# Attention scores as plain float32 products on two row groups of TensorE, in place of split float32r parts

## The chip, the cores and the metric

The kernel runs on one core of a Trainium2 chip. The metric is device time in microseconds. The run before was timed three times: 2007.59, 2006.73 and 2007.32 us, median 2007.32.

The engines are called as in the profile: PE is TensorE's matrix products, PEld its weight loads, DVE VectorE, ACT ScalarE, POOL GpSimd, and SP the queue that issues most DMAs.

## What is computed

One inference step of a two-layer backbone for 384 tokens: 256 latent tokens and 128 context tokens, 1024 channels. Each layer has a SwiGLU feed-forward block, a token-mixing block and a second feed-forward block, all with normalisation and modulation from a conditioning vector. The mixing block has a gated spatial branch and an attention branch. The attention branch is the one that changes:

```python
def diff_attention(q, k, v, lam):
    ...
    def block(qi):
        s = jnp.einsum('bqhid,bkhid->bihqk', qi, k).astype(jnp.float32) * scale
        p = jax.nn.softmax(s, axis=-1)
        a = p[:, 0] - lam * p[:, 1]
        return jnp.einsum('bhqk,bkhe->bqhe', a.astype(v.dtype), v)
```

There are 8 heads of 128 channels. A head has two halves `i` of 64 channels. Each half gives its own scores and softmax; the second softmax, times `lam`, is taken from the first. Latent queries see 128 cached context keys and 256 latent keys, 384 in all. Context queries see the 128 context keys alone. Latent queries and keys are turned by a rotary product first.

## The kernel before, in words

Activations are kept transposed, with channels on the partitions and the 384 tokens along the row. Weights stream in from HBM in pairs of chunks of 1 MB, issued by SP (`load_next`). Each 128x1024 chunk is split into two float32r parts, `whi` by ACT (L173) and `wlo` by DVE (L176). A projection (`col_job`) goes over 8 weight tiles of 128x128 and makes three float32r products for each (`mm3`: L226 `whi` by `h_hi`, L227 `wlo` by `h_hi`, L228 `whi` by `h_lo`).

The order of the work is written by hand. A job is a generator that yields after each weight tile. `fill(n)` runs the next n tiles of the queue of jobs.

Attention is cut in 48 units over the two layers: 8 heads by 3 groups of 128 queries. Two of the three groups are latent queries with 384 keys (called long units below), the third is context queries with 128 keys (short units). The table `ORDER` says what runs between the units' phases; `F` entries are fills, so projections of the next heads and of the gates run beside attention:

```python
ORDER = [(c[0], int(c[1:])) for c in "S0 F1 B0 T1 F3 E0 C0 O2 F4 P1 F1 X2".split()]
```

- `phase_s` (S) makes the scores of one unit in a PSUM tile `sc` of two halves with 512 columns each, and DVE takes the maximum (L943, L944). The tile has one buffer.
- `phase_e` (E) is the exponential on ACT (L953). `phase_c` (C) joins the two halves on DVE (L962 to L965).
- `phase_t` (T, L974), `phase_p` (P, L990), `phase_o` (O) and `phase_x` (X, L1013) transpose, multiply by the values, normalise and transpose back, for units one or two steps older.
- B, after the third unit of a head, runs the jobs up to the next head's projections and calls `build` for it.

`q_evac` and `k_evac` take the projections of one head out of PSUM into `qf` and `kf` and apply the rotary product (`rope`, L769 to L772). `k_evac` also loads the cached keys beside them (L785). `build` then splits both into float32r parts, two halves by five operations: four on ACT in all (L802, L804), six on DVE (L803, L805, L807). Tile `qa` holds, for a half, the 64 rows of the high part beside the 64 rows of the low part; `ka` holds the high part of the keys twice; `kl` their low part. So the first score product of a half (L940) goes over 128 rows and the second (L941) over 64:

```python
T.matmul(sc[:, i, 0:nk], lhsT=qa[h][:, i, js], rhs=ka[h][:, i, keys], start=True, stop=False)
T.matmul(sc[:, i, 0:nk], lhsT=qa[h][rows, i, js], rhs=kl[h][rows, keys], start=False, stop=True)
```

Three places with plain float32 products are in the kernel already and are used below for comparison. L990 is the product with the values. L415 (`mod_piece`) and L463 (`mod_piece_v`) make the modulation; they cut the array in four column groups of 32 weight columns by `tile_position`. L415 makes four products, one on each group, for each of 8 channel tiles. L463 makes four products in all, one on each group.

Of the kernel before, what the change touches and what calls it, by code (L numbers as in the profile page):

```python
# [9 lines left out]
F32 = mybir.dt.float32  # L10
F32R = mybir.dt.float32r
AF = mybir.ActivationFunctionType
ALU = mybir.AluOpType
# [25 lines left out]
def hybrid_step(  # L39
# [19 lines left out]

# [1 line left out]
    ident = cp.tile([P, P], F32, name="ident")  # L61
# [22 lines left out]

# [1 line left out]
    # A job is a generator that yields after each 128x128 weight tile. Weights come in pairs of  # L86
    # chunks (1 MB each pair); a chunk is 8 tiles, split into two float32r parts when it is near.
    jobs = []
# [18 lines left out]
    def plan_order():  # L107
        seen = set()
        upto = 0

        def see(key):
            if key not in seen:
                seen.add(key)
                order.append(key)

        for j in jobs:
            for m in j.mods:
                see(m)
            if j.n:
                lim = min(len(chunks), j.first + max(j.n, 1) + W_BUFS - 1)  # L120
                if j.n > W_BUFS:
                    lim = min(len(chunks), j.first + W_BUFS)
                while upto < lim:
                    see(chunks[upto][:-1])
                    upto += 1
                # later chunks of a long job
                while upto < min(len(chunks), j.first + j.n + W_BUFS - 1):
                    see(chunks[upto][:-1])
                    upto += 1
# [27 lines left out]
    def run_later(n=1):  # L157
        # what was put off by some tiles of work, in order
        for e in later:
            e[0] -= n  # L160
        while later and later[0][0] <= 0:
            later.pop(0)[1]()
# [60 lines left out]

# [1 line left out]
    def mm3(ps, w_hi, w_lo, r_hi, r_lo, first, last):  # L225
# [38 lines left out]
    def start_group(keys, rhs, evacs, make):  # L264
        # The first products, while the first modulation comes in by quarters (two k-tiles each).
        q_keys = [[("w_mod0", n, q) for n in range(2)] for q in range(4)]
# [124 lines left out]

    # modulation: one piece (1024 columns) of silu(cond) @ w_mod + b_mod
    def mod_keys(l, pc):
# [11 lines left out]
    def mod_piece(l, pc):  # L405
        # The four column groups of the array work on 256 columns each.
        big = pp.tile([P, 2, 512], F32, tag="sc", name="sc")
# [31 lines left out]
    def mod_piece_v(l, pc):  # L439
        # the products on the vector engine, the sum over partitions on the tensor engine  # L440
        acc0 = sp.tile([P, 1024], F32, tag="KA", name="acc0")
        acc1 = [sp.tile([P, 512], F32, tag=t, name="acc1") for t in ("KL", "kf")]
        parts = [(0, slice(0, 1024), acc0), (1, slice(0, 512), acc1[0]), (1, slice(512, 1024), acc1[1])]
# [37 lines left out]
    class Mods:  # L481
        # modulation pieces cut in steps, put between other jobs
        def __init__(self, pieces=(), pieces_v=()):
# [34 lines left out]

# [1 line left out]
    nst = {}  # L520
# [13 lines left out]
    def rsqrt(v, w, E):  # L534
        # r = v**-0.5, with a Newton step on the engine E
        r = tiny(w, "yr")
# [43 lines left out]
    def make_h(l, i, pc_sh):  # L580
# [9 lines left out]
        def make(kt, ahead=2):  # L590
            # h of k-tile kt; the part that needs no bias runs two tiles ahead
            for k2 in range(kt, min(kt + ahead, KD)):
# [24 lines left out]
    def norm_job(make, mods):  # L617
        # the first products of mods run while the norm is worked out
        steps = [mods.take() for _ in range(3)]
# [18 lines left out]

# [1 line left out]
    def ffn(l, i, w13, w2, mods, first=3):  # L640
# [60 lines left out]

# [1 line left out]
    def mixer(l, mods):  # L703
# [60 lines left out]

        qf, kf, qa, ka, kl, vc = {}, {}, {}, {}, {}, {}

# [7 lines left out]
        def q_evac(h):  # L774
            def e(ps):
                qf[h] = sp.tile([P, NT], F32, tag="qf", name="qf")
                S.activation(out=qf[h], in_=ps, func=AF.Copy)
                rope(qf[h][:, LATS])
            return e

        def k_evac(h):
            # the keys of a head: cached, latent, context
            def e(ps):
                t = sp.tile([P, 512], F32, tag="kf", name="kf")
                nc.sync.dma_start(out=t[:, 0:P], in_=a["cache_k"][l, h])  # L785
                S.activation(out=t[:, P:512], in_=ps, func=AF.Copy)
                nc.sync.dma_start(out=a["new_k"][l, h], in_=t[:, 384:512])
                rope(t[:, P:384])
                kf[h] = t
                if h == 0:  # L790
                    bg.append(lambda: build(0))
            return e

        def build(h):
            # float32r parts: 64 rows of a half of the head, beside them the rows of the other part
            q, k = qf.pop(h), kf.pop(h)
            qa[h] = sp.tile([P, 2, NT], F32R, tag="QA", name="QA")
            ka[h] = sp.tile([P, 2, 512], F32R, tag="KA", name="KA")
            kl[h] = sp.tile([P, 512], F32R, tag="KL", name="KL")
            lower, upper = slice(0, 64), slice(64, 128)  # L800
            for i, own, oth in ((0, lower, upper), (1, upper, lower)):
                S.activation(out=qa[h][own, i, :], in_=q[own, :], func=AF.Copy)  # L802
                V.tensor_copy(out=ka[h][own, i, :], in_=k[own, :])  # L803
                S.activation(out=ka[h][oth, i, :], in_=k[own, :], func=AF.Copy)  # L804
                V.tensor_tensor(  # L805
                    out=qa[h][oth, i, :], in0=q[own, :], in1=qa[h][own, i, :].bitcast(F32), op=ALU.subtract)
                V.tensor_tensor(  # L807
                    out=kl[h][own, :], in0=k[own, :], in1=ka[h][own, i, :].bitcast(F32), op=ALU.subtract)
            vc[h] = sp.tile([P, P], F32, tag="vc", name="vc", bufs=2)
            nc.sync.dma_start(out=vc[h], in_=a["cache_v"][l, h])  # L810

# [15 lines left out]
        def gate_evac(which, f):  # L827
            def e(ps):
# [4 lines left out]
                else:  # L833
                    if f % 2 == 0:
                        tg["t"] = sp.tile([P, 2, NT], F32, tag="QA", name="tg")
                    t = tg["t"][:, f % 2, :]
# [22 lines left out]

        # w_in pairs: u 0-3, zv 4-7, (q,k) 8-15, v 16-19, g_a 20-23, g_b 24-27  # L860
        def wk(pair, half):
# [21 lines left out]
        col_job(wk(8, 1), rhs_h, k_evac(0))  # L883
        # zv and v share a slot, so the spatial gate is through before v is written
        vk = [wk(16 + i // 2, i % 2) for i in range(8)]
# [4 lines left out]

        # what the tensor engine does beside the attention
        side = []
# [4 lines left out]
        while side or hq < NH:  # L897
            # the next head's projections end shortly before its scores
            if hq < NH and (not side or pos + 8 > PER_HEAD * hq - 28):
# [27 lines left out]

# [1 line left out]
        units = [(h, j) for h in range(NH) for j in range(3)]  # L929
        us = {}  # L930

        def phase_s(n):
# [3 lines left out]
            sc = pp.tile([P, 2, 512], F32, tag="sc", name="sc")  # L936
            js = slice(j * P, (j + 1) * P)
            for i in range(2):
                rows = slice(i * 64, (i + 1) * 64)
                T.matmul(sc[:, i, 0:nk], lhsT=qa[h][:, i, js], rhs=ka[h][:, i, keys], start=True, stop=False)  # L940
                T.matmul(sc[:, i, 0:nk], lhsT=qa[h][rows, i, js], rhs=kl[h][rows, keys], start=False, stop=True)  # L941
            mx = tiny(2, "ym")
# [77 lines left out]
        def attention():  # L1020
            nu = len(units)
            for n in range(nu + 3):
                for what, arg in ORDER:
# [6 lines left out]
                    if what == "B":  # L1030
                        h = units[u][0] + 1
                        if units[u][1] == 2 and h < NH:
                            run_until(qk_job[h])
                            build(h)
                        continue
# [16 lines left out]
    def lambdas():  # L1052
        lamb = nst.pop("lamb")
        # -lambda per layer
        lp = tmp(256).rearrange("p (l r d) -> p l r d", l=2, r=2)
# [11 lines left out]

# [1 line left out]
    marks = []  # L1069
# [18 lines left out]
    with tc.manual_schedule():  # L1088
# [23 lines left out]
        run_later(99)  # L1112
        # final norm
        norm_stats0()
# [11 lines left out]
def _cols(w, n0, n):  # L1126
    # (L, 8*128, N) columns n0..n0+n -> (L, n/256, 128, 2*8*128): pairs of column tiles
    L = w.shape[0]
# [4 lines left out]
def _rows(w, n0):  # L1133
    # (L, 1024, N) columns n0..n0+1024 -> (L, 4, 128, 4*512): halves of 512 columns, by 4 k-tiles
    L = w.shape[0]
# [66 lines left out]
```

## Time and profile before

| | |
|---|---|
| median of three timed runs | 2007.32 us |
| span of the profiled execution | 2006.0 us |
| PE busy | 1971.3 us, 98% |
| DVE busy | 1211.9 us, 60% |
| ACT busy | 830.1 us, 41% |
| POOL busy | 149.4 us, 7% |
| moved by DMA | 308.66 MB, 154 GB/s |

The profile is of one execution. Its own time is given as the span from its first to its last instruction, 2006.0 us; no other time stands beside it. The timed median is 1.3 us above that.

The page lists busy time by engine, then 40 slices of the span, then groups of instructions. The trace behind it can be asked for a timeline of one engine, for groups by line and form, and for the busy time of each engine in a stretch. Matmuls overlap in the records, so that the duration of one (0.34 us for 384 columns) is longer than the distance between the starts of two; distances between starts tell the pace. A plain float32 product of two 4-byte operands stands in the trace as two records of PE and two weight loads, a float32r product as one of each.

### The profile page before, as it was taken

To read this page: it belongs to the slowest core of one execution; us is meant where nothing else is said; L and a number is where in the kernel's file an instruction comes from. 1 tells how busy PE (TensorE), PEld (TensorE's weight loads), DVE (VectorE), ACT (ScalarE), POOL (GpSimd) and SP (SyncE) were. 2 spreads that over 40 slices of the span, in tenths; PEclk is the share of its full clock that TensorE was granted. 3 is DMA by queue.
4 is the path that set the end of the run, shared out by engine and by line. 5 is a ranking of instruction groups with operands and counts; after the bars stand their busy time and mean duration, and the time that the engine had idled before them with its cause. 6 is when DMAs were issued, how large, how long until landed. Compare 5 with 4: busy or idle time off the path is not lost. (4 is left out here: it accounts for less than half of the span.)

```text
span 2006.0 us, 28427 instructions
## 1 busy us (share of the span) xinstructions
PE 1971.3 (98%) x11442; PEld 1873.7 (93%) x11442; DVE 1211.9 (60%) x1942; ACT 830.1 (41%) x1484; POOL 149.4 (7%) x407
## 2 busy tenths in 40 slices
PE   7999999999999999999999999999999999999997
PEld 5999998888999999999999999989898999999997
DVE  5757685368874565667556577445688645544433
ACT  4433324446663353333343333253566533533321
POOL 0000000003441000000000000000144300000000
PEclk9999999999999999999999999999999999999999
DMA  8645556533233344545554455453323233533330
GB/s 327 212 154 184 182 224 220 189 121 105 85 111 106 126 166 170 189 168 189 178 181 167 168 189 196 166 180 122 121 76 113 102 123 122 189 124 127 125 124 32
DMA packets 52115, 308.66 MB, mean 154 GB/s; under 512 B 6416, under 2 KB 13968, under 8 KB 15632
## 3 DMA queue, kind: packets, MB, share of 16 engines
q1 hardware_dynamic: 51552, 306.74, 42.7%
q8 instruction: 90, 1.47, 0.3%
q14 instruction: 41, 0.34, 0.0%
q10 hardware_dynamic: 432, 0.11, 0.0%
HBM read 303.16 MB, written 3.67 MB: 153 GB/s over the span
## 5 line engine op out<-in xcount | busy, mean ns | idle before, releaser
L176 DVE TENSOR_TENSOR wlo<-raw,whi 128x1024 fp32r<-128x1024 f32 x424 | 517.7, 1224 | 345.8 <-ACT whi L173 345.7
L226 PE MATMUL mm<-h_hi,whi 128*128 128x384 f32 x2048 | 702.5, 343 | 3.9 <-ACT h_hi L602 3.9
L228 PE MATMUL mm<-h_lo,whi 128*128 128x384 f32 x2048 | 689.1, 336 | 0.6
L227 PE MATMUL mm<-h_hi,wlo 128*128 128x384 f32 x2048 | 688.3, 336 | 0.0
L173 ACT ACTIVATE whi<-raw 128x1024 fp32r<-128x1024 f32 x424 | 444.7, 1052 | 227.7 <-PE mm L228 147.3
L226 PEld LDWEIGHTS mm<-h_hi,whi 128*128 128x128 f32 x2048 | 384.4, 188 | 19.2 <-ACT h_hi L602 6.9
L228 PEld LDWEIGHTS mm<-h_lo,whi 128*128 128x128 f32 x2048 | 384.4, 188 | 2.5 <-DVE h_lo L605 2.4
L227 PEld LDWEIGHTS mm<-h_hi,wlo 128*128 128x128 f32 x2048 | 384.8, 188 | 0.2
L226 PE MATMUL mm<-S,whi 128*128 128x384 f32 x1088 | 370.2, 340 | 0.0
L228 PE MATMUL mm<-S,whi 128*128 128x384 f32 x1088 | 365.7, 336 | 0.0
L227 PE MATMUL mm<-S,wlo 128*128 128x384 f32 x1088 | 365.6, 336 | 0.0
L226 PEld LDWEIGHTS mm<-S,whi 128*128 128x128 f32 x1088 | 204.1, 188 | 6.6 <-issue 6.1
L227 PEld LDWEIGHTS mm<-S,wlo 128*128 128x128 f32 x1088 | 204.2, 188 | 0.0
L228 PEld LDWEIGHTS mm<-S,whi 128*128 128x128 f32 x1088 | 204.1, 188 | 0.0
L383 ACT ACTIVATE S<-t 128x384 fp32r<-128x384 f32 x104 | 54.6, 525 | 318.5 <-DVE t L664 280.8
L455 DVE SCALAR_TENSOR_TENSOR acc<-raw,scond,acc 128x512 f32<-128x512 f32 (+1 forms) x210 | 182.4, 925 | 0.0
L664 DVE TENSOR_TENSOR t<-t,mm 128x384 f32<-128x384 f32 x88 | 48.7, 554 | 122.3 <-PE mm L228 120.5
L538 POOL TENSOR_TENSOR yr<-yv,nhalf 128x3 f32<-128x3 f32 x9 | 7.7, 855 | 1515.1 <-DVE yv L564 1393.9
L656 ACT ACTIVATE t<-mm 128x384 f32<-128x384 f32 x88 | 43.2, 490 | 168.0 <-PE mm L228 167.9
L386 DVE TENSOR_TENSOR S<-t,S 128x384 fp32r<-128x384 f32 x104 | 58.1, 558 | 60.9 <-ACT S L383 60.9
L363 PE MATMUL mm<-whi,h_hi 128*128 128x512 f32 x192 | 77.2, 402 | 1.4 <-ACT S L820 1.4
L364 PE MATMUL mm<-wlo,h_hi 128*128 128x512 f32 x192 | 75.2, 392 | 0.0
(143 smaller groups left out, 1513.0 us busy)
## 6 DMA issues: line engine op xcount, KB each, us to landing
raw<-in_ffn_w SPq DMA_DIRECT2D x132, 1024.0 KB, 4.9
raw<-in_w_mod SPq DMA_DIRECT2D x68, 1024.0 KB, 5.0
raw<-in_w_in SPq DMA_DIRECT2D x56, 1024.0 KB, 4.9
raw<-in_w_branch_a SPq DMA_DIRECT2D x8, 1024.0 KB, 5.0
raw<-in_w_branch_b SPq DMA_DIRECT2D x8, 1024.0 KB, 5.0
raw<-in_w_out SPq DMA_DIRECT2D x8, 1024.0 KB, 4.9
S<-in_w_mod SPq DMA_DIRECT2D x4, 1024.0 KB, 14.7
x<-in_x SPq DMA_DIRECT2D x4, 384.0 KB, 4.2
```

The lines of the kernel that those rows point to most:

```text
L173: S.activation(out=hi, in_=raw, func=AF.Copy)
L176: V.tensor_tensor(out=lo, in0=raw, in1=hi.bitcast(F32), op=ALU.subtract)
L226: T.matmul(ps, lhsT=w_hi, rhs=r_hi, start=first, stop=False)
L227: T.matmul(ps, lhsT=w_lo, rhs=r_hi, start=False, stop=False)
L228: T.matmul(ps, lhsT=w_hi, rhs=r_lo, start=False, stop=last)
L363: T.matmul(ps, lhsT=l_hi[:, kt, ts_], rhs=hi[:, sl], start=first, stop=False)
L364: T.matmul(ps, lhsT=l_hi[:, kt, ts_], rhs=lo[:, sl], start=False, stop=False)
L383: S.activation(out=dst_hi, in_=src, func=AF.Copy)
L386: V.tensor_tensor(out=dst_lo, in0=src, in1=dst_hi.bitcast(F32), op=ALU.subtract)
L455: V.scalar_tensor_tensor(out=acc, in0=src, scalar=s, in1=acc, op0=ALU.mult, op1=ALU.add)
L656: S.activation(out=s, in_=ps, func=AF.Silu)
L664: V.tensor_tensor(out=s, in0=s, in1=ps, op=ALU.mult)
```

## The change

The split of q and k is gone. The scores of each half are one plain float32 product from `qf` and `kf`, over the 64 rows of that half: partitions 0 to 63 for the first, 64 to 127 for the second. `qf` and `kf` get two buffers, since they are now read until a head's last scores. The load of the cached values moves from `build` to `k_evac`. The gate tile `tg` takes a buffer of tag `e` instead of `QA`, and the accumulators of `mod_piece_v` take the two buffers of `kf` instead of one each of `KL` and `kf`. Comments are removed as well; the core of the diff is:

```diff
@@ mod_piece_v
-        acc1 = [sp.tile([P, 512], F32, tag=t, name="acc1") for t in ("KL", "kf")]
+        acc1 = [sp.tile([P, 512], F32, tag="kf", name="acc1", bufs=2) for _ in range(2)]
@@ mixer
-                qf[h] = sp.tile([P, NT], F32, tag="qf", name="qf")
+                qf[h] = sp.tile([P, NT], F32, tag="qf", name="qf", bufs=2)
...
-                t = sp.tile([P, 512], F32, tag="kf", name="kf")
+                t = sp.tile([P, 512], F32, tag="kf", name="kf", bufs=2)
                 nc.sync.dma_start(out=t[:, 0:P], in_=a["cache_k"][l, h])
+                vc[h] = sp.tile([P, P], F32, tag="vc", name="vc", bufs=2)
+                nc.sync.dma_start(out=vc[h], in_=a["cache_v"][l, h])
...
-                if h == 0:
-                    bg.append(lambda: build(0))
             return e
-        def build(h):
-            q, k = qf.pop(h), kf.pop(h)
-            qa[h] = sp.tile([P, 2, NT], F32R, tag="QA", name="QA")
-            ka[h] = sp.tile([P, 2, 512], F32R, tag="KA", name="KA")
-            kl[h] = sp.tile([P, 512], F32R, tag="KL", name="KL")
...
-            vc[h] = sp.tile([P, P], F32, tag="vc", name="vc", bufs=2)
-            nc.sync.dma_start(out=vc[h], in_=a["cache_v"][l, h])
...
-                        tg["t"] = sp.tile([P, 2, NT], F32, tag="QA", name="tg")
+                        tg["t"] = sp.tile([P, 2, NT], F32, tag="e", name="tg", bufs=2)
...
             for i in range(2):
                 rows = slice(i * 64, (i + 1) * 64)
-                T.matmul(sc[:, i, 0:nk], lhsT=qa[h][:, i, js], rhs=ka[h][:, i, keys], start=True, stop=False)
-                T.matmul(sc[:, i, 0:nk], lhsT=qa[h][rows, i, js], rhs=kl[h][rows, keys], start=False, stop=True)
+                T.matmul(sc[:, i, 0:nk], lhsT=qf[h][rows, js], rhs=kf[h][rows, keys], start=True, stop=True)
...
                             run_until(qk_job[h])
-                            build(h)
```

On PE, at the first unit of attention in layer 0, the order was this (`sc` the score tile, `mm` a projection's accumulator, `KA`, `QA` and `KL` the tiles of `ka`, `qa` and `kl`):

```order
L228 MATMUL mm<-h_lo,whi 128x384
L940 MATMUL sc<-KA,QA 128x384
L941 MATMUL sc<-KL,QA 128x384
L940 MATMUL sc<-KA,QA 128x384
L941 MATMUL sc<-KL,QA 128x384
L226 MATMUL mm<-h_hi,whi 128x384
```

and is now:

```order
L226 MATMUL mm<-h_hi,whi 128x384
L227 MATMUL mm<-h_hi,wlo 128x384
L228 MATMUL mm<-h_lo,whi 128x384
L923 MATMUL sc<-kf,qf 128x384 x2
L226 MATMUL mm<-h_hi,whi 128x384
```

Four instructions in a row have become two, at the same place between two weight tiles; all 48 units read so. The shape in a row is that of the output.

On DVE, after the third unit's scores of head 0, the order was:

```order
L943 TENSOR_REDUCE ym<-sc 128x2
L944 TENSOR_SCALAR ym<-ym 128x2
L176 TENSOR_TENSOR wlo<-raw,whi 128x1024
L803 CAST KA<-kf 64x512
L805 TENSOR_TENSOR QA<-qf,QA 64x384
L807 TENSOR_TENSOR KL<-kf,KA 64x512
L803 CAST KA<-kf 64x512
L805 TENSOR_TENSOR QA<-qf,QA 64x384
L807 TENSOR_TENSOR KL<-kf,KA 64x512
L962 RECIPROCAL yc<-yz 128x1
```

and is now:

```order
L772 TENSOR_TENSOR kf<-kf,t 128x256
L925 TENSOR_REDUCE ym<-sc 128x2
L926 TENSOR_SCALAR ym<-ym 128x2
L176 TENSOR_TENSOR wlo<-raw,whi 128x1024
L944 RECIPROCAL yc<-yz 128x1
```

The six operations of `build` are gone there, and the head's keys are ready with the last rotary operation (L772), ahead of the third unit's maximum.

On SP, for head 0 of a layer, the order was:

```order
L785 DMA kf<-in_cache_k 128x128
L787 DMA out_new_k<-kf 128x128
L141 DMA raw<-in_w_in 128x2048 x2
L810 DMA vc<-in_cache_v 128x128
L822 DMA out_new_v<-S_3613 128x512
```

and is now:

```order
L141 DMA raw<-in_w_in 128x2048 x7
L785 DMA kf<-in_cache_k 128x128
L787 DMA vc<-in_cache_v 128x128
L789 DMA out_new_k<-kf 128x128
L141 DMA raw<-in_w_in 128x2048 x2
L804 DMA out_new_v<-S_3600 128x512
```

The load of the cached values has moved past two weight loads and the store of the new keys, to directly behind the cached keys.

## Rows read from the trace of the kernel before

**Rows 1.** The page of the profile: its span, and its busy time by engine.

```profile
span 2006.0 us, 28427 instructions
...
PE 1971.3 (98%) x11442; PEld 1873.7 (93%) x11442; DVE 1211.9 (60%) x1942; ACT 830.1 (41%) x1484; POOL 149.4 (7%) x407
```

**Rows 2.** Busy time by stretch: attention of layer 0, columns in the first line.

```profile
core 0: us, PE busy (x) PEld busy (x) DVE busy (x) ACT busy (x) POOL busy (x), PEclk, DMA share, GB/s
445.20:607.00 161.80, 161.80 (x907) 145.85 (x906) 127.18 (x283) 105.98 (x279) 62.86 (x178) 1.00 0.28 95
```

**Rows 3.** Groups by line and form: the second score product of each half.

```profile
L941 PE MATMUL sc<-KL,QA 64*128 64x384 f32 x64 | 28.0, 437 | 0.0
...
L941 PE MATMUL sc<-KL,QA 64*128 64x128 f32 x32 | 10.4, 324 | 0.0
```

**Rows 4.** PE's timeline, a long unit: start us, duration us, engine, line, operation.

```profile
445.09 0.34 PE L228 MATMUL mm<-h_lo,whi 128*128 128x384 f32 x1
445.26 0.34 PE L940 MATMUL sc<-KA,QA 128*128 128x384 f32 x1
445.53 0.44 PE L941 MATMUL sc<-KL,QA 64*128 64x384 f32 x1
445.90 0.44 PE L940 MATMUL sc<-KA,QA 128*128 128x384 f32 x1
446.27 0.44 PE L941 MATMUL sc<-KL,QA 64*128 64x384 f32 x1
446.63 0.44 PE L226 MATMUL mm<-h_hi,whi 128*128 128x384 f32 x1
446.91 0.34 PE L227 MATMUL mm<-h_hi,wlo 128*128 128x384 f32 x1
```

**Rows 5.** PE's timeline, a short unit.

```profile
562.67 0.31 PE L940 MATMUL sc<-KA,QA 128*128 128x128 f32 x1
562.91 0.32 PE L941 MATMUL sc<-KL,QA 64*128 64x128 f32 x1
563.16 0.33 PE L940 MATMUL sc<-KA,QA 128*128 128x128 f32 x1
563.42 0.32 PE L941 MATMUL sc<-KL,QA 64*128 64x128 f32 x1
563.67 0.45 PE L226 MATMUL mm<-S,whi 128*128 128x384 f32 x1
```

**Rows 6.** PE's timeline in three pieces: products on four column groups.

```profile
120.28 0.64 PE L463 MATMUL sc<-acc,ones 128*32 128x512 f32 x4
...
120.74 0.61 PE L463 MATMUL sc<-acc,ones 128*32 128x512 f32 x4
...
121.28 0.44 PE L226 MATMUL mm<-h_hi,whi 128*128 128x384 f32 x1
```

**Rows 7.** PE's timeline in two pieces: the modulation products, 256 columns.

```profile
317.14 0.61 PE L415 MATMUL sc<-raw,scond 128*32 128x256 f32 x8
...
317.57 0.40 PE L415 MATMUL sc<-raw,scond 128*32 128x256 f32 x4
```

**Rows 8.** The weight loads' timeline behind a long unit.

```profile
446.63 0.19 PEld L226 LDWEIGHTS mm<-h_hi,whi 128*128 128x128 f32 x1 [0.18 <-issue]
446.74 0.19 PEld L227 LDWEIGHTS mm<-h_hi,wlo 128*128 128x128 f32 x1
```

**Rows 9.** Groups by line and form: two of the operations that split k.

```profile
L807 DVE TENSOR_TENSOR KL<-kf,KA 64x512 fp32r<-64x512 f32 x32 | 22.0, 687 | 1.0
...
L804 ACT ACTIVATE KA<-kf 64x512 fp32r<-64x512 f32 x32 | 20.2, 630 | 0.8
```

**Rows 10.** Timelines of DVE, PE and ACT: what stands closest before scores.

```profile
464.15 0.69 DVE L807 TENSOR_TENSOR KL<-kf,KA 64x512 fp32r<-64x512 f32 x1
...
465.42 0.42 PE L940 MATMUL sc<-KA,QA 128*128 128x384 f32 x1
...
561.01 0.20 ACT L953 ACTIVATION_READ_ACCUMULATOR e<-sc,ym 128x1 f32 x1
```

More of the change, by code (lines that the diff above doesn't have):

```diff
@@ L763, in flush_bg @@
             run_later(99)
-        qf, kf, qa, ka, kl, vc = {}, {}, {}, {}, {}, {}
+        qf, kf, vc = {}, {}, {}
         def rope(lat):
@@ L789, in e @@
                 kf[h] = t
-                if h == 0:
-                    bg.append(lambda: build(0))
-            return e
-        def build(h):
-            q, k = qf.pop(h), kf.pop(h)
-            qa[h] = sp.tile([P, 2, NT], F32R, tag="QA", name="QA")
-            ka[h] = sp.tile([P, 2, 512], F32R, tag="KA", name="KA")
-            kl[h] = sp.tile([P, 512], F32R, tag="KL", name="KL")
[L800 to L808, printed above, removed]
-            vc[h] = sp.tile([P, P], F32, tag="vc", name="vc", bufs=2)
-            nc.sync.dma_start(out=vc[h], in_=a["cache_v"][l, h])
+            return e
         def v_evac(hf):
```

## The prediction, made before the changed kernel was run

> **What bounds the kernel now.** I read the head of the page first. The span is 2006.0 us and TensorE is busy in 98% of it, VectorE in 60% [rows 1]. A busy TensorE in this profile may still be waiting inside the modelled length of a matmul, so the second view is the stretch in which attention runs in layer 0, 445.2 to 607.0 us. There PE is busy for 161.80 of 161.80 us at a granted clock of 1.00, which is its 2.4 GHz level, while DVE does 127.18 us and ACT 105.98 us of work [rows 2]. Layer 1 repeats the stretch from 1429 us. So nothing but PE's own pace matters here: what shortens its instruction stream shortens the run, and what is taken from ACT or DVE does not.
>
> The third view, the groups by line and form, gives the counts. The second score product stands 64 times with 384 keys and 32 times with 128 [rows 3]. There are two halves in each unit, so 32 long units (latent queries) and 16 short ones (context queries).
>
> The fourth view is PE's timeline through one unit. Here the reader should look at distances between starts, not at durations. An ordinary 384-column product follows the last in 0.17 us (445.09 to 445.26). The four score products do not keep that step: from L940 to L941 it is 0.27, then 0.37, 0.37, and 0.36 to the next projection product [rows 4]. They alternate between 128 and 64 array rows, and each change of shape makes the array empty itself and load its weights in the open. The short unit shows the same with 0.25, 0.26 and 0.25 [rows 5]. A short product therefore gains almost nothing from being short; the changes of shape are the price.
>
> **The change part by part.**
>
> *The score products.* Each unit loses four float32r products and gets two plain float32 ones, rows 0 to 63 and rows 64 to 127, both of 64-row shape. The changes of shape fall from four to two: one on the way in, one on the way out. The way in costs 0.27 less 0.17, 0.10 us, before and after alike, so it drops out of the difference. The way out is inside the step from L941 to L226.
>
> How long does a plain float32 product run? The trace has some on column groups of the array. L415 sends 256 columns; from 317.14 to 317.57 lie two rounds of it, 0.215 us each, so 0.107 per 128 columns and 0.32 for 384 [rows 7]. Each plain product is two such records: the ten calls of L463 make four products each, and its two rounds hold eight records. A float32r product is one record; half of the plain record's length, 0.16 for 384 columns, fits the ordinary step of 0.17.
>
> How do two products on different groups of the array run? No row has two row groups side by side, so this is the open cost. The nearest row is L463, four products on four column groups: four records start together at 120.28, the other four together at 120.74, and the next projection starts at 121.28 [rows 6]. So all first records run at once, then all second ones. I take the row groups to do the same, because these are also separate parts of the array, and because the two halves go to different halves of the PSUM tile.
>
> Then the pair of a long unit takes the step from L941 to L226, 0.37, with its one pass of 0.16 replaced by two rounds of 0.32: 0.37 - 0.16 + 0.64 = 0.85 us. What it replaces is L940's own step of 0.17 and the steps 0.37, 0.37 and 0.36, 1.27 us. The saving is 0.42. In a short unit the pair takes 0.25 - 0.05 + 0.21 = 0.41; it replaces 0.06 (a third of 0.17) + 0.25 + 0.26 + 0.25 = 0.82. The saving is 0.41. Together 32 x 0.42 + 16 x 0.41 = 13.4 + 6.6 = 20.0 us.
>
> The bounds of the two costs taken by analogy: load and way out of L463's eight records are 1.00 less two passes of 0.43, 0.14, where I took 0.37 - 0.16 = 0.21. That end gives 0.07 x 48 = 3.4 us more gain. The other end is that the two halves' weights load one after the other: a load of 128 columns takes 0.11 (446.63 to 446.74 [rows 8]), so 0.11 x 48 = 5.3 us less gain, and 10.6 us less if the second round's loads stand open too. I keep the middle, since its 0.21 comes from a 64-row product with 128 weight columns, the very shape that stays.
>
> Here a rule of the Trainium skill speaks against me. Its page "TensorE: Matmul & The Clock Gate", Part 3 ("What overlaps and what doesn't") says that matmuls keep program order in start and in end. Each product's two records are neighbours in the program; by that rule the second record of the lower half starts ahead of the first of the upper half, and the pair takes three rounds instead of two, which would make the sum 1999.2. [Rows 6] differ from it for column groups, and the measurement decides there. The same part states 3.07 times the speed for four row groups in use at once; no run here shows it.
>
> *The splitting of q and k* (`build`) goes: per head four activations and six DVE operations, 16 times, such as 32 of 0.630 us on ACT and 32 of 0.687 us on DVE [rows 9]. I price it at nothing, since PE never idles in the stretch [rows 2]. It was close to being seen: for head 1 the last DVE operation of the split starts at 464.15 and takes 0.69, and the head's first scores start at 465.42 [rows 10]. This margin of 0.58 us now grows, because the scores wait for the rotary products and the cached keys alone, which had to be there before the split.
>
> *What is late next?* The score tile has one buffer, so a unit's scores wait until ACT's exponentials have read the last unit's. They end at 561.21 (561.01 + 0.20 [rows 10]) and the next scores start at 562.67 [rows 5], a margin of 1.46 us. What PE does between the end of one unit's scores and the start of the next is the same as before, so a shorter pair does not eat into it.
>
> *Buffers and DMAs.* The load of the cached values moves from `build` to `k_evac`, on SP between the load of the cached keys and the store of the new ones. It waits for a slot last read two heads earlier, so the store and the weight loads behind it are not held. q and k get two buffers, the gate tile takes a slot of the exponentials, and the vector engine's modulation accumulators take the two slots of k. None of these is waited for by PE now. Nothing for all of them; the cover is the same full PE.
>
> **The sum.** 2006.0 - 20.0 = 1986.0 us of span. The median of the three timed runs, 2007.32, is 1.3 us above the profiled span; with that added, **1987.3 us**. Its own range, by the bounds above, is 1984 to 1993.
>
> **The rivals.**
>
> *Three rounds.* The lower half's second record goes ahead of the upper half's first, so only the middle round is shared. It costs one round more: 32 x 0.32 + 16 x 0.107 = 11.9 us, that is 1999.2 us. For it: the two records of a product are issued together. Against it: [rows 6].
>
> *Turn-taking, the rival on the other side.* The two row groups do not run at once, because both write all 128 partitions of PSUM, which L463's groups (32 partitions each) never do. Then a pair takes four rounds, two more than forecast: 2 x 11.9 = 23.9 us, 2011.2 us. If in addition the weights of a 64-row product can load only when the array is empty, as every L941 shows now [rows 4], three more loads of 0.11 stand open in each unit: 3 x 0.11 x 48 = 15.8 us, 2027 us. It decides from the point at which a long pair takes more than 1.27 us. For it: every 64-row product in this trace runs alone. Against it: those stand between 128-row ones, which explains the open load.
>
> *The change is not what it says*, for instance if both halves were placed on the same rows. The slices are those that L941 uses today, partitions 0 to 63 and 64 to 127, so I give this little; it would be turn-taking in its effect.
>
> **How the numbers follow.** The forecast gets 0.73, three rounds 0.11, turn-taking 0.13 (0.05 for the bare 2011 us, 0.08 with loads in the open), anything else 0.03, spread evenly. A measurement of this kernel can tell about 0.2% from no change, 4 us: below 2003.3 is faster, above 2011.3 slower. Faster is 0.73 + 0.11 + 0.01 = 0.85; no change 0.05 + 0.01 = 0.06; slower 0.08 + 0.01 = 0.09. The range runs from 1982, a little under the lower bound, to 2000, which takes in three rounds and the open loads (1998); turn-taking stays outside.
>
> **What would show it.** In PE's timeline of the changed kernel a long unit should show two score records starting together, the other two 0.32 to 0.43 us later, and the next projection product 0.85 us after the first; a short one 0.41. A third start time means three rounds; four starts spaced by 0.32 or 0.43 mean turn-taking. The attention stretch should shorten by 10 us in each layer, with PE still without idle time, and with ACT and DVE less busy. The forecast is wrong if a pair takes over 1.0 us, or if PE shows a wait for ACT or a DMA ahead of the scores.

## The result, and the profile after

The changed kernel takes 1987.07 us (median of 4 runs, 1984.65 to 1990.18), the kernel before beside it 2007.45 us. The ratio is 0.9897, with a 95% interval of 0.9883 to 0.9912. The forecast was 1987.3 us. Where the changed kernel is timed again below, one run of its four, 2139.03 us at a mean granted clock of 0.849 against 0.995 or more, is a slow one and is left out.

The page of the changed kernel begins with its span and, by engine, busy time, share of the span and count; the lines answer to [rows 1]:

```profile
span 1986.9 us, 28281 instructions
...
PE 1953.6 (98%) x11442; PEld 1855.4 (93%) x11442; DVE 1159.9 (58%) x1846; ACT 796.1 (40%) x1420; POOL 134.4 (7%) x407
```

PE's count is the same as before, 11442: 192 float32r score records went and 192 records of plain float32 products came. So the gain is not in a shorter list. DVE and ACT lost 96 and 64 instructions, the split.

The busy time by stretch, from the first score product to the last one of layer 0 and of layer 1. Columns are the stretch, its length, then busy time and count for each engine, the granted clock, the DMA share and GB/s. First the kernel before:

```profile
core 0: us, PE busy (x) PEld busy (x) DVE busy (x) ACT busy (x) POOL busy (x), PEclk, DMA share, GB/s
445.26:605.08 159.82, 159.82 (x895) 143.98 (x894) 125.37 (x279) 104.62 (x277) 61.36 (x172) 1.00 0.28 97
1428.91:1588.71 159.80, 159.80 (x895) 143.96 (x894) 125.36 (x279) 104.61 (x277) 61.69 (x172) 1.00 0.28 97
```

and the changed kernel:

```profile
445.82:595.27 149.45, 149.45 (x895) 133.66 (x894) 102.87 (x236) 89.22 (x248) 53.35 (x171) 1.00 0.30 103
1419.21:1568.66 149.45, 149.45 (x895) 133.67 (x894) 102.86 (x236) 89.22 (x248) 53.68 (x171) 1.00 0.30 103
```

The same 895 matmul records of PE, busy all the time and at the 2.4 GHz level in both, take 10.4 us less in each layer. That makes 20.7 us. The spans differ by 19.1; the other 1.6 us were lost outside these two stretches, the first 0.56 of it before the first score product (445.82 against 445.26). The four runs of the changed kernel spread over 5.5 us, so I look no further into it, and what cost the 1.6 us stays open.

PE's timeline at the first long unit (columns: start us, duration us, engine, line, operation), to be held against [rows 4]:

```profile
445.56 0.34 PE L228 MATMUL mm<-h_lo,whi 128*128 128x384 f32 x1
445.83 0.92 PE L923 MATMUL sc<-kf,qf 64*128 64x384 f32 x4
446.67 0.45 PE L226 MATMUL mm<-h_hi,whi 128*128 128x384 f32 x1
446.96 0.34 PE L227 MATMUL mm<-h_hi,wlo 128*128 128x384 f32 x1
```

The same four records, looked at from their beginning and from their end:

```profile
445.83 0.59 PE L923 MATMUL sc<-kf,qf 64*128 64x384 f32 x2
...
446.25 0.49 PE L923 MATMUL sc<-kf,qf 64*128 64x384 f32 x2
```

And a short unit, to be held against [rows 5]:

```profile
458.13 0.34 PE L228 MATMUL mm<-h_lo,whi 128*128 128x384 f32 x1
458.40 0.49 PE L923 MATMUL sc<-kf,qf 64*128 64x128 f32 x4
458.82 0.44 PE L226 MATMUL mm<-h_hi,whi 128*128 128x384 f32 x1
```

Two records start at 445.83 and two at 446.25: two start times, not three or four. The way in is 0.27 (445.56 to 445.83). The pair, to the next projection product, is 0.84 in the long unit and 0.42 in the short one.

These two units stand directly behind a projection product, as 6 of the 48 do; before the other 42 a transposing product (L995) stands between. The saving is the same there: by the starts in both traces, from the product ahead of the scores to the second projection product behind them, a long unit is 0.44 us shorter on average and a short one 0.41.

### The profile page after: what moved, and what is told of

It reads as the page before. It is cut to its first block, busy times and chain, and to the rows that moved or that the text cites. A ratio compares the mean times of both kernels' runs of the same rounds, so it can differ in the third digit from the quotient of the medians.

```text
span 1986.9 us, 28281 instructions
## 1 busy us (share of the span) xinstructions
PE 1953.6 (98%) x11442; PEld 1855.4 (93%) x11442; DVE 1159.9 (58%) x1846; ACT 796.1 (40%) x1420; POOL 134.4 (7%) x407
## 4 chain that ended last, share of the span: by engine, by line
PE 82%; issue 15%; DVE 1%; ACT 1%; POOL 0%; DMA 0%; POOLq 0%; DVEq 0%; ACTq 0%
PE mm L226 23%; PE mm L228 23%; PE mm L227 23%; PE mm L363 2%; PE mm L365 2%; PE mm L364 2%; PE sc L923 2%; PE mm L972 1%; PE sc L415 1%; PE tp L956 1%; PE sc L278 1%; PE sc L463 1%; PE tp L749 1%; PE ms L575 0%; POOL yr L538 0%
## 5 line engine op out<-in xcount | busy, mean ns | idle before, releaser
L365 PE MATMUL mm<-whi,h_lo 128*128 128x512 f32 x192 | 75.3, 392 | 0.0
```

Source lines behind the costliest of these rows:

```text
L365: T.matmul(ps, lhsT=l_lo[:, kt, ts_], rhs=hi[:, sl], start=False, stop=last)
```

## Experiments

My theory has three parts: PE's own pace sets the time; what costs in the score products is each change between the 128-row and the 64-row shape; and the two row groups run at once. The rivals were that row groups add nothing, that the plain form or fewer instructions make the gain, and that the work taken from ACT and DVE does. Five more kernels tell these apart, and two kernels are timed once more.

**Both halves on the same rows.** The changed kernel without the second row group (half of the scores is left out):

```diff
-                rows = slice(i * 64, (i + 1) * 64)
-                T.matmul(sc[:, i, 0:nk], lhsT=qf[h][rows, js], rhs=kf[h][rows, keys], start=True, stop=True)
+                T.matmul(sc[:, i, 0:nk], lhsT=qf[h][0:64, js], rhs=kf[h][0:64, keys], start=True, stop=True)
```

> The changed kernel with both score products on array rows 0 to 63, so that they cannot run at once; it computes the second half's scores from the first half's channels, so that half of the scores is left out. Everything else is as in the changed kernel. My theory (the two row groups run at once): a pair now takes four rounds, 0.84 + 0.64 = 1.48 us in a long unit and 0.41 + 0.21 = 0.62 in a short one, and the time rises by 32 x 0.64 + 16 x 0.21 = 23.9 us over the changed kernel's 1987.1, to about 2011, which is as slow as the kernel before. Rival (the gain came from fewer changes of shape and fewer instructions, the row groups add nothing): the time stays at 1987.

Measured: 2011.63 us, ratio to the kernel before 1.0015 (1.0006 to 1.0025). PE's timeline at a long unit of this kernel:

```profile
448.70 0.34 PE L228 MATMUL mm<-h_lo,whi 128*128 128x384 f32 x1
448.97 1.55 PE L922 MATMUL sc<-kf,qf 64*128 64x384 f32 x4
450.45 0.44 PE L226 MATMUL mm<-h_hi,whi 128*128 128x384 f32 x1
```

The four records now run one behind the other: 1.48 us to the next projection product in place of 0.84, with 0.43, 0.32 and 0.32 between their starts. All of the gain is gone and a little more. Plain float32 products by themselves, though half as many instructions in the program and with half the changes of shape, are no faster than the four float32r products. The second row group is what pays.

**The old products, grouped by shape.** The kernel before, with the order of its four products changed and nothing else:

```diff
             for i in range(2):
-                rows = slice(i * 64, (i + 1) * 64)
                 T.matmul(sc[:, i, 0:nk], lhsT=qa[h][:, i, js], rhs=ka[h][:, i, keys], start=True, stop=False)
+            for i in range(2):
+                rows = slice(i * 64, (i + 1) * 64)
                 T.matmul(sc[:, i, 0:nk], lhsT=qa[h][rows, i, js], rhs=kl[h][rows, keys], start=False, stop=True)
```

> The kernel before with its four float32r score products grouped by shape: the two over 128 rows first, then the two over 64 rows, one on each row group. Nothing else is changed; the split stays. My theory (each change of shape costs about 0.2 us on PE, and two 64-row products on two row groups run at once): the long unit's scores to the next projection product take 0.17 + 0.17 + 0.10 + 0.37 = 0.81 us in place of 1.37, the short unit's 0.11 + 0.11 + 0.10 + 0.25 = 0.57 in place of 0.92, so 32 x 0.56 + 16 x 0.35 = 23.5 us less than before, about 1984, 3 us under the changed kernel. If float32r products on two row groups take turns, a long pair costs 0.16 and a short one 0.05 more, 5.9 us in all: about 1990. Rival (the plain float32 form itself, or the split that it saves, is what made the kernel faster): the time stays at 2007.

Measured: 1984.59 us, ratio 0.988 (0.9865 to 0.9894). PE's timeline at its first long unit:

```profile
443.75 0.34 PE L228 MATMUL mm<-h_lo,whi 128*128 128x384 f32 x1
443.93 0.51 PE L939 MATMUL sc<-KA,QA 128*128 128x384 f32 x2
444.37 0.44 PE L942 MATMUL sc<-KL,QA 64*128 64x384 f32 x2
444.74 0.44 PE L226 MATMUL mm<-h_hi,whi 128*128 128x384 f32 x1
```

From 443.93 to 444.74 it is 0.81 us, as expected, against 1.37 in [rows 4]. The two 64-row products start together at 444.37 and take 0.37, what one alone took before. The busy time by stretch, from its first score product to its last in layer 0:

```profile
443.93:591.66 147.73, 147.73 (x895) 138.11 (x894) 124.14 (x278) 104.13 (x276) 63.10 (x171) 1.00 0.30 105
```

A change of order gives the whole gain, without plain float32 and with the split still there. The 2.5 us under the changed kernel are not clear of noise by the times alone, since the two intervals overlap; the stretch is 1.7 us shorter (147.73 against 149.45). So the gain needs neither the plain form nor the saved split.

**The split kept as idle work.** The changed kernel, with `build` back at its old places; it writes into tile `KA`, which nothing reads:

```diff
+                if h == 0:
+                    bg.append(lambda: build(0))
...
+        def build(h):
+            q, k = qf[h], kf[h]
+            ka = sp.tile([P, 2, 512], F32R, tag="KA", name="KA")
+            lower, upper = slice(0, 64), slice(64, 128)
+            for i, own, oth in ((0, lower, upper), (1, upper, lower)):
+                S.activation(out=ka[own, i, 0:NT], in_=q[own, :], func=AF.Copy)
+                V.tensor_copy(out=ka[own, i, :], in_=k[own, :])
+                S.activation(out=ka[oth, i, :], in_=k[own, :], func=AF.Copy)
...
                             run_until(qk_job[h])
+                            build(h)
```

> The changed kernel with the split's operations put back as idle work at the same places: per head four on ACT and six on DVE, into one tile that nothing reads. My theory (the split was hidden behind a full PE): 1987, within 2 us of the changed kernel. Rival (part of the gain came from the work taken from ACT and DVE): the time rises toward 2007; if ACT's and DVE's 90 us counted at a tenth, by 9 us.

Measured: 1989.02 us, ratio 0.9905 (0.989 to 0.992). The changed kernel gave 0.9897 and, timed again below, 0.9899; the interval here and that of the first timing (0.9883 to 0.9912) overlap. The busy time by stretch, from its first score product to its last in layer 0:

```profile
444.97:594.51 149.54, 149.54 (x894) 133.74 (x894) 124.11 (x278) 103.52 (x276) 63.17 (x171) 1.00 0.30 103
```

Against the changed kernel DVE does 21.2 us more here and ACT 14.3 us more, and the stretch is 0.09 us longer. The split was hidden, and costs nothing that can be told when it is put back.

**The low keys padded to 128 rows.** The kernel before, with the low part of the keys in a tile `klz` of two halves, whose other 64 rows are set to zero once. The result is the same sum. Room for it comes from one buffer of tag `e` instead of two, from `bb` in tag `KA`, and from one accumulator of the modulation in tag `QA`:

```diff
+    klz = cp.tile([P, 2, 512], F32R, name="klz")
...
-                    out=kl[h][own, :], in0=k[own, :], in1=ka[h][own, i, :].bitcast(F32), op=ALU.subtract)
+                    out=klz[own, i, :], in0=k[own, :], in1=ka[h][own, i, :].bitcast(F32), op=ALU.subtract)
...
-                T.matmul(sc[:, i, 0:nk], lhsT=qa[h][rows, i, js], rhs=kl[h][rows, keys], start=False, stop=True)
+                T.matmul(sc[:, i, 0:nk], lhsT=qa[h][:, i, js], rhs=klz[:, i, keys], start=False, stop=True)
...
+        for i, oth in ((0, slice(64, 128)), (1, slice(0, 64))):
+            for c0 in (0, 256):
+                V.tensor_copy(out=klz[oth, i, c0:c0 + 256], in_=z[oth, 0:256])
```

> The kernel before with the low part of the keys padded to 128 rows by zeros, so that all four float32r score products have the 128-row shape and PE never changes shape for them. To make room, the exponentials have one buffer instead of two and two tiles share other slots. My theory (the price is the changes of shape): a long unit's scores take four ordinary steps, 0.69 us in place of 1.47 (with the slow step behind them), a short unit's 4 x 0.11 + 0.10 = 0.53 in place of 1.03; 32 x 0.78 + 16 x 0.5 = 33 us less than before, about 1974, 13 us under the changed kernel. Rival 1 (the score products cost what they cost by number of passes, not by shape): 2007. Rival 2 (with one buffer, the exponentials come late and PE waits): PE idle in the attention stretch, and the time above 1974 by as much.

Measured: 1975.29 us, ratio 0.9834 (0.9819 to 0.9848). PE's timeline at its first long unit, then at a short one:

```profile
445.06 0.34 PE L939 MATMUL sc<-KA,QA 128*128 128x384 f32 x1
445.23 0.34 PE L940 MATMUL sc<-klz,QA 128*128 128x384 f32 x1
445.41 0.33 PE L939 MATMUL sc<-KA,QA 128*128 128x384 f32 x1
445.58 0.34 PE L940 MATMUL sc<-klz,QA 128*128 128x384 f32 x1
445.76 0.34 PE L227 MATMUL mm<-h_hi,whi 128*128 128x384 f32 x1
...
456.99 0.22 PE L939 MATMUL sc<-KA,QA 128*128 128x128 f32 x1
457.05 0.27 PE L940 MATMUL sc<-klz,QA 128*128 128x128 f32 x1
457.16 0.28 PE L939 MATMUL sc<-KA,QA 128*128 128x128 f32 x1
457.27 0.27 PE L940 MATMUL sc<-klz,QA 128*128 128x128 f32 x1
457.39 0.39 PE L227 MATMUL mm<-h_hi,whi 128*128 128x384 f32 x1
```

The four products go at the ordinary step, 0.70 us in all (445.06 to 445.76), with the same passes over the array as in [rows 4]; only the shape differs. The order is the old one too, two products in a row into each half of `sc`, so the long steps before were no wait of the second product for the sums of the first. In the short unit the step is 0.06 from the first product to the second, and 0.11 after that. The busy time by stretch in layer 0:

```profile
445.05:588.12 143.07, 143.07 (x895) 141.51 (x894) 123.16 (x278) 103.24 (x276) 66.97 (x171) 1.00 0.31 108
```

PE has no idle time, so the single buffer of exponentials is not waited for (rival 2). This kernel is faster than the changed one and the grouped one; the intervals lie apart.

**The room alone.** The kernel before, with only the buffers moved as above:

```diff
-        acc1 = [sp.tile([P, 512], F32, tag=t, name="acc1") for t in ("KL", "kf")]
+        acc1 = [sp.tile([P, 512], F32, tag=t, name="acc1") for t in ("QA", "kf")]
...
-            m["bb"] = sp.tile([P, 4, P], F32, tag="e", name="bb", bufs=2)
+            m["bb"] = sp.tile([P, 4, P], F32, tag="KA", name="bb")
...
-            e = sp.tile([P, 2, NT], F32, tag="e", name="e", bufs=2)
+            e = sp.tile([P, 2, NT], F32, tag="e", name="e", bufs=1)
```

> The kernel before with nothing but the room made for the padded keys: one buffer of exponentials instead of two, two tiles in other slots; the score products are untouched. My theory (these slots are waited for by nobody while PE is full): 2007 to 2009, as the kernel before beside it, so that the padded kernel's gain is that of its products alone. Rival (the single buffer costs or gives time of its own): a difference of over 2 us, by which the padded kernel's gain would be wrong.

Measured: 2009.47 us beside 2008.59 us of the kernel before, ratio 1.0006 (0.9997 to 1.0015). The moved buffers do nothing that can be told.

**The changed kernel and the padded one, once more, on one chip.** Both as above, with no edit.

> The changed kernel once more, on one chip with the padded one. My theory: 1987, as first timed (1984.7 to 1990.2). If the first timing was off, this shows by how much; the kernel with the split kept gave 1989.0, so a value of 1987 to 1989 means that the split costs nothing that can be told, one of 1980 that it costs.

> The padded kernel beside the changed one. My theory (a change of shape costs PE about 0.2 us, and without one four float32r products take 0.69 us against 1.05 for the plain pair): 12 us under the changed kernel, by 32 x 0.36 + 16 x 0.1 = 13 us in the score products. Rival (the difference of the first call was between chips or calls): under 5 us.

Measured: 1988.37 us for the changed kernel (median of three runs), 0.9899 of the 2008.59 us of the kernel before beside it, and 1975.94 us for the padded one, ratio 0.9839 (0.9826 to 0.9852). The padded kernel is 12.4 us under the changed one, where 12 to 13 were expected.

## Why the prediction was right

*The bound.* PE's pace alone was to matter, and nothing taken from ACT or DVE. Right, and shown twice: the stretch shortened by 10.4 us a layer with PE full in both, and the split put back changed it by 0.09 us.

*The open cost, how two row groups run.* It was taken from four column groups [rows 6], and row groups behave alike: two records at 445.83, two at 446.25. The rule that I weighed against this, in the Trainium skill's page "TensorE: Matmul & The Clock Gate", Part 3 ("What overlaps and what doesn't"), would have the lower half's second record start ahead of the upper half's first. The trace does not agree, if the two records of a product are neighbours in the program, as the prediction took them to be: two records start together, 0.42 us ahead of the other two. These two belong to different halves, since on the same rows no two records of a long unit start less than 0.32 us apart (first experiment). The trace gives start times and not the order in the program, so the rule itself is not refuted. With three rounds the pair would have taken 0.32 us more, and it took 0.84. Turn-taking is excluded by the same rows, and the first experiment shows what it would have cost: 1.48 us a long unit and 2011.63 us, where the prediction had 2011.2 for the bare form.

*The sizes.* The pair was put at 0.85 and 0.41, and measures 0.84 and 0.42. The way in was put at 0.27 in all, and measures 0.27. The loads of the two halves do not stand in the open one after the other, which was the upper bound. The gain inside attention was put at 20.0 us and is 20.7; the long units gave 0.44 us each where 0.42 was put. That the total came out closer still, 1987.07 for 1987.3, is partly luck: the profiled run lost 1.6 us outside attention, which the prediction did not have, and its own time, 1988.66, lies 1.8 us over its span where I had added 1.3.

*Where the gain comes from.* The prediction put it on the changes of shape falling from four to two and on the row groups. The experiments weigh the two. Fewer changes without the second row group gave nothing (2011.63), because the plain form needs four rounds of 0.32 where the old products needed four of about 0.16. The row groups halve that. Grouping the old products gave a little more than the change, 1.7 us a layer in the stretch, since these have half the length and as few changes of shape. And with no change of shape at all the old products gave the most.

*What stayed hidden, as priced.* The margin of the single score tile held, since PE has no idle time in the stretch. The moved load of the cached values, the second buffers and the other slots show no wait of PE: the list of its waits over the whole run has no entry that the kernel before lacks. I did not try them one by one.

## What to carry to other kernels

On a full PE, read the distances between starts and look for the products that do not keep the step; here every change between array shapes cost about 0.2 us in a long unit and 0.14 in a short one (the kernel before against the padded one, over four changes), more than the product itself (0.17 and 0.11). Group the products of one shape, give two half-height products two row groups side by side, or pad the short one with zeros to full height: on this kernel the padding was best, by 12.4 us over plain float32 on two row groups. Work taken from engines that are not the bound gave nothing here that can be told, even 86 us of it (52.0 on DVE and 34.0 on ACT by the two pages).

## What the runs showed of the hardware

A float32r product of 128 columns that follows one of 384 columns hands on after 0.06 us, a third of the 0.17 (456.99 to 457.05 in the padded kernel). Further ones behind it step at 0.11 us (457.05, 457.16, 457.27, 457.39); that is also the distance between the starts of two loads of 128 weight columns [rows 8]. The prediction put L940's own step in a short unit at a third of 0.17, the expectations of the experiments put every short product at 0.11. The trace bears out the prediction: a short unit became 0.41 us shorter, as forecast.
